# Where a hybrid encoder layer scales its softmax and splits the gate's weights, and how it loads p

## The chip, the core and the metric

The kernel runs on one core of a Trainium2 chip. A core has five engines with an instruction queue each: TensorE (PE in the profile, with its weight loads shown apart as PEld), VectorE (DVE), ScalarE (ACT), GpSimd (POOL) and SyncE (SP, which here only issues DMAs). Each engine works through its own queue in order; semaphores hold an instruction until what it needs is there. The metric is the device time of one execution in microseconds (us).

## The reference

One encoder layer on x (1024 tokens, width 1024), everything in float32:

```python
u = x @ w_in                                   # rq, rk, rv, rg, aq, ak, av
y_ret = retention(rq, rk, rv) -> group norm -> * silu(rg)      # 8 heads, both directions, chunks of 128
y_att = windowed_gqa(aq, ak, av, sink)         # 8 query heads, 2 key heads, +-128 tokens, softmax with a sink
h = LN1(alpha * x + concat(y_ret, y_att) @ w_out)
ffn = (silu(h @ w_gate) * (h @ w_up)) @ w_down                 # hidden width 2816
out = LN2(alpha * h + ffn + sigmoid(h @ w_pg) * (p @ w_pe))    # p: 1024 x 256
```

## The kernel before

Full-precision products are made from three matmuls in a reduced format: an operand x is split into `hi` (ACT copies x into the format) and `lo` (DVE computes x - hi), and a product is hi·hi + hi·lo + lo·hi. `split` (lines 72 to 74) is the ACT and DVE pair, `mm3` (76 to 79) and `mm3c` (840 to 842) are the three matmuls. A filler step below is one `mm3` with 512 columns.

The work comes in stages. (1) First projections with all PSUM banks. (2) The mixer: five calls of `run`, whose list gives PE's order by hand: operations of attention and retention for one pair of heads, and between them `None` entries, each of which stands for a portion of filler (the remaining projection matmuls, from `queue`). First come two lists for attention pair 0 alone (4 portions, 16 filler steps; then more than 20 portions, 64 steps), then retention 0 alone (14 portions, 48 steps), then pairs 1 to 3, where retention and attention go together (28 portions, 48 steps each). In the mixer only PE's order is written by hand; a planner orders ACT, DVE, POOL and SP by its own estimate of when each operand is there, in program order where several are ready. (3) The output projection and LN1. (4) The gate products and embeddings, below. (5) The gate/up products, and (6) the down products, with the order of all engines written by hand.

Softmax (lines 476 to 501, one block of 128 queries and two heads at a time): PE makes the scores, DVE adds the position term and takes the maximum (L493), ACT takes exp with the sum (L497), DVE the reciprocal (L499) and DVE scales the tile (L501). Later PE transposes it (L509) and ACT evicts the transpose (L511). There are 32 such blocks, so 64 scales.

The presplit (lines 535 to 583) prepares operands for stage 4: w_pg in seven combinations (a fast product scheme with seven in place of eight block products, 4 row blocks each, 28 in all), w_pe (4) and p (4). Each is loaded into a tile `pre`, some are summed in place (L561, 16 sums), split into a tile `pro` (two buffers) and stored to DRAM (`pgd`, `ped`, `ptd`). It begins with retention 0: `run` takes one of its 36 steps after each portion of filler. A block's two loads are in the same step as its first split.

Stage 4 computes seven products (`product`, L851 to 863; each with four rows k of 128 tokens and four weight blocks kt that `stream` loads from `pgd` into eight buffers of tags `w` and `u`) and sixteen embeddings (`embed`, L868 to 883): a load of p (L872, tile `p`, two buffers, 256 KB), six matmuls, a sigmoid of the gate's sum (L878), a product (L879) and an addition to `accs` (L881). Four embeddings follow the second product, eight are put between the rows of the last one, and four follow it. PE's order here is the planner's. Tiles of tag `ln` (two buffers) are used by `t_sums` before, which makes sums of h, and by the weights of stage 5 after (L952).

Tile `raw` has two buffers, through which most weights come before they are split: `w_mt` (filler tiles), `w_rv` (eight loads, L322, in the first list of the mixer).

Of the kernel before, what the change touches and what calls it, by code (L numbers as in the profile page):

```python
# [9 lines left out]
F32 = mybir.dt.float32  # L10
F32R = mybir.dt.float32r
AF = mybir.ActivationFunctionType
ALU = mybir.AluOpType
# [27 lines left out]
def layer(tc, xT, xn, w_first, w_mt, w_rv, w_out, w_pg, w_pe, pT, w_gu, w_dn,  # L41
# [30 lines left out]
    def split(raw, hi, lo):  # L72
        act.activation(hi, raw, AF.Copy)  # L73
        dve.tensor_tensor(lo, raw, hi.bitcast(F32), ALU.subtract)  # L74

    def mm3(o, lh, ll, rh, rl, start, stop):
        pe.matmul(o, lh, rh, start=start, stop=False)  # L77
        pe.matmul(o, lh, rl, start=False, stop=False)  # L78
        pe.matmul(o, ll, rh, start=False, stop=stop)  # L79

    last = {}

# [386 lines left out]
    class Attention:  # L469
# [6 lines left out]
        def scores(self, n):  # L476
            i, qs = self.i, self.qs
            hh, j = divmod(n, 4)
            if j == 0:
                self.st[hh] = bt([P, 4, 4, 2], "st", 2)  # L480
            st_ = self.st[hh]
            lo, hi = span(n)
            nk = (hi - lo) * P
            tc0 = C_BASE + (lo - n + 1) * P
            qc = slice(n * P, (n + 1) * P)
            sc = self.sc[n] = [bt([P, NKT + 4], "sc", NSC) for _ in range(2)]
            for g in range(2):
                pool.tensor_copy(sc[g][:, nk:nk + 1], skb[:, 2 * i + g:2 * i + g + 1])  # L488
            for g in range(2):
                b = bank("s")  # L490
                pe.matmul(b[:, :nk], qs[g][:, qc], k1[g][:, lo * P:hi * P], start=True, stop=False)
                pe.matmul(b[:, :nk], qs[g][:, qc], kz[g][:, lo * P:hi * P], start=False, stop=True)  # L492
                dve.tensor_tensor_reduce(sc[g][:, :nk], cst[:, tc0:tc0 + nk], b[:, :nk], slope(i, g),  # L493
                                         skb[:, 2 * i + g:2 * i + g + 1], ALU.add, ALU.max, st_[:, 0, j, g:g + 1])
            dve.tensor_scalar(st_[:, 1, j, :], st_[:, 0, j, :], -1.0, None, ALU.mult)  # L495
            for g in range(2):
                act.activation(sc[g][:, :nk + 1], sc[g][:, :nk + 1], AF.Exp, bias=st_[:, 1, j, g:g + 1],  # L497
                               accum_out=st_[:, 2, j, g:g + 1])
            dve.reciprocal(st_[:, 3, j, :], st_[:, 2, j, :])  # L499
            for g in range(2):  # L500
                dve.tensor_scalar(sc[g][:, :nk], sc[g][:, :nk], st_[:, 3, j, g:g + 1], None, ALU.mult)  # L501

        def turn(self, n):
            lo, hi = span(n)
# [27 lines left out]
    ped = dr.tile([2, 2, P, 2, HF], F32, name="ped")  # L532
    ptd = dr.tile([4, P, 2, HF], F32, name="ptd")

    def presplit():

        raw = [a_tile([P, 2, HF], "pre", "A1") for _ in range(2)]
        ops = [a_tile([P, 2, HF], "pro", "A1", F32R) for _ in range(2)]
        n = [0]

        def put(x, dst):
            o = ops[n[0] % 2]
            n[0] += 1
            split(x, o[:, 0, :], o[:, 1, :])
            sp.dma_start(dst, o.bitcast(F32))

        def load(k):
            for j in range(2):
                sp.dma_start(raw[j], w_pg[j, k])

        def gate_steps(k):

            (a11, a21), (a12, a22) = ([raw[j][:, i, :] for i in range(2)] for j in range(2))
            tt = dve.tensor_tensor

            def s(p, x, *sums):
                def f():
                    if p == 1:
                        load(k)
                    for a in sums:  # L560
                        tt(*a)  # L561
                    put(x, pgd[p - 1, k])
                return f

            return [s(1, a11), s(4, a22), s(2, a12), s(5, a22, (a22, a21, a22, ALU.add)),
                    s(7, a21, (a21, a11, a21, ALU.subtract)), s(6, a11, (a11, a22, a11, ALU.subtract)),
                    s(3, a12, (a12, a12, a11, ALU.subtract))]

        def pe_steps(h):
            def f(q):  # L570
                if q == 0:
                    sp.dma_start(raw[h], w_pe[h].rearrange("p (q c) -> p q c", q=2))
                put(raw[h][:, q, :], ped[h, q])
            return [lambda q=q: f(q) for q in range(2)]

        def p_steps(j):
            def f():
                x = raw[j // 2][:, j % 2, :]
                for i in range(2):
                    sp.dma_start(x[:, i * 2 * P:(i + 1) * 2 * P], pT[2 * j + i])  # L580
                put(x, ptd[j])
            return [f]

        return [f for k in range(4) for f in gate_steps(k)] + [f for h in range(2) for f in pe_steps(h)] + \
            [f for j in range(4) for f in p_steps(j)]

    side = []

# [32 lines left out]
    def run(steps, total):  # L621

        shares = steps.count(None)
        done = n = 0
        for f in steps:
            if f is None:
                n += 1
                take(total * n // shares - done)
                done = total * n // shares
                if side:  # L630
                    side.pop(0)()
            else:
                f[0](*f[1:])

    F = None
    with tc.manual_schedule(engines={mybir.EngineType.PE}):
        enqueue([mtile(0, ev_av), proj_rv(), *project(1), *project(2), *project(3), gate(0), gate(1), gate(2), gate(3)])
        a = Attention(0, ytile(1))
        sco, trn, val = (lambda n: (a.scores, n)), (lambda n: (a.turn, n)), (lambda n: (a.values, n))
        run([F, F, sco(0), F, sco(1), F], 16)  # L640
        run([F, (av_turn, 0), F, trn(0), (av_turn, 1), F, sco(2), F, trn(1), F, sco(3), F, val(0), val(1), F, trn(2), F,
             sco(4), F, trn(3), F, sco(5), F, val(2), val(3), F, trn(4), F, sco(6), F, trn(5), F, sco(7), F, val(4), val(5),
             F, trn(6), F, trn(7), F, val(6), val(7), F], 64)
        side.extend(presplit())
        r = Retention(0, ytile(0))
        K, C, N = (lambda q: (r.keys, q)), (lambda q: (r.kv, q)), (lambda q: (r.norm, q))
        Q, X = (lambda q: (r.scores, q)), (lambda q: (r.turn, q))
        Y = lambda hh, k: (r.out, hh, (2 * k, 2 * k + 1))
        run([K(0), F, C(0), K(1), F, C(1), K(2), F, Q(0), C(2), K(3), F, C(3), (r.scan,), F, F, F,
             Y(0, 0), F, Y(0, 1), N(0), F, Q(1), F, F, Y(1, 0), F, Y(1, 1), N(1), F, F], 48)  # L650
        for i in range(1, NPAIR):
            if i == 2:
                while side:
                    side.pop(0)()
            X0, X1 = X(0), X(1)
            r = Retention(i, ytile(2 * i))
            a = Attention(i, ytile(2 * i + 1))
            run([K(0), Q(0), F, X0, F, C(0), F, X1, K(1), F, C(1), sco(0), F,
                K(2), F, C(2), sco(1), F, K(3), F, trn(0), sco(2), F, C(3), (r.scan,), F, trn(1), F,
                sco(3), F, val(0), val(1), F, trn(2), Y(0, 0), F, sco(4), F, Y(0, 1), N(0), trn(3), F, sco(5), F,  # L660
                val(2), val(3), Q(1), F, trn(4), F, F, sco(6), F, trn(5), F, Y(1, 0), F, sco(7), F, val(4), val(5), F,
                Y(1, 1), N(1), trn(6), F, trn(7), F, F, val(6), val(7)], 48)
        run([F, X(0), F, X(1), F, F], 16)
# [192 lines left out]
    def four(k):  # L856
        return [bank(t) for t in sets[k]]

    def product(p, banks, first, stat, side=()):

        w = [stream(pgd[p - 1, kt]) for kt in range(4)]
        for k in range(4):
            c = slice(k * P, (k + 1) * P)
            for kt in range(4):
                mm3c(banks[k], stat[:, 0, kt, c], stat[:, 1, kt, c], w[kt][:, 0, :], w[kt][:, 1, :], first and kt == 0, kt == 3)
            if k < len(side):
                side[k]()

    def embed(t, h, x, wpe, tag):

        pt = ct([P, 2, 2 * P], "p", 2, F32R)
        sp.dma_start(pt.bitcast(F32), ptd[t // 2][:, :, (t % 2) * 2 * P:(t % 2 + 1) * 2 * P])  # L872
        b2 = bank(tag)
        for q in range(2):
            c = slice(q * P, (q + 1) * P)
# [19 lines left out]
    to_hT(4)  # L895
    to_hT(5)
    X = four("a")
    product(1, X, True, HB[0, 0], [lambda t=t: to_hT(t) for t in (6, 7)])
    s1 = [r[:, i * HF:(i + 1) * HF] for r in (rawt(2 * HF), rawt(2 * HF)) for i in range(2)]
    for k in range(4):  # L900
        act.activation(s1[k], X[k], AF.Copy)
# [15 lines left out]
    product(4, Y, False, TT[4])  # L917
    add4(s1, s1, Y)
    wpe = [stream(ped[1, q]) for q in range(2)]
    both_ = [pair_of(lambda k=k: embed(k, 1, s1[k], wpe, "mm"), lambda k=k: embed(4 + k, 1, c22[k], wpe, "s")) for k in range(4)]  # L920
    product(3, Z, False, HB[1, 1], both_)
    wpe0 = [stream(ped[0, q]) for q in range(2)]
    for k in range(4):
# [545 lines left out]
```

## Time and profile before

| | |
|---|---|
| Median of three runs | 1227.47 us (1227.15 to 1230.7) |
| Profiled execution, whole | 1230.34 us |
| Its span, first to last instruction | 1228.6 us |
| PE busy | 1201.0 us, 98% of the span |
| DVE, ACT, POOL busy | 751.0, 480.3, 364.4 us |
| Mean granted clock of TensorE | 0.993 |

The profile is of one execution. "L73" is line 73 of the kernel; tile names are the program's, with buffer numbers left out (`bmm`, `bs`, `bt`, `bo` are PSUM banks of four tags). A row such as `PE bt L370 <- DVE kv L388: 3.3, 2, 2.4` says that instructions of line 370 on PE waited for line 388 on DVE: in total, how often, the longest. A row of the timeline gives start, length, engine, line, operation, output and input tiles, shape, count and, in brackets, the idle time of the engine just before it with what ended it. A matmul's length is longer than the distance between two starts, since matmuls are pipelined; the distance is what one costs.

### The profile page before, as it was taken

To read this page: it belongs to the slowest core of one execution; us is meant where nothing else is said; L and a number is where in the kernel's file an instruction comes from. 1 tells how busy PE (TensorE), PEld (TensorE's weight loads), DVE (VectorE), ACT (ScalarE), POOL (GpSimd) and SP (SyncE) were. 2 spreads that over 40 slices of the span, in tenths; PEclk is the share of its full clock that TensorE was granted. 3 is DMA by queue.
4 is the path that set the end of the run, shared out by engine and by line. 5 is a ranking of instruction groups with operands and counts; after the bars stand their busy time and mean duration, and the time that the engine had idled before them with its cause. 6 is when DMAs were issued, how large, how long until landed. Compare 5 with 4: busy or idle time off the path is not lost.

```text
span 1228.6 us, 16503 instructions
## 1 busy us (share of the span) xinstructions
PE 1201.0 (98%) x5939; PEld 993.8 (81%) x5939; DVE 751.0 (61%) x1326; ACT 480.3 (39%) x896; POOL 364.4 (30%) x342
## 2 busy tenths in 40 slices
PE   9999989999999999999999999999999999999996
PEld 7888878788887888787788888888888888888885
DVE  5542869766755396944755544555545556875677
ACT  5633336544565114301433232332323334562453
POOL 2000010201110020000556656456465523034232
PEclk9999999999999999999999999999999999999999
DMA  6311545710103314566532133322233149999976
GB/s 253 95 35 52 206 165 230 257 35 18 35 18 121 102 52 159 201 205 220 208 129 78 71 110 129 129 78 82 99 129 129 69 147 288 387 277 218 256 175 197
DMA packets 69970, 179.50 MB, mean 146 GB/s; under 512 B 8064, under 2 KB 13312, under 8 KB 69888
## 3 DMA queue, kind: packets, MB, share of 16 engines
q1 hardware_dynamic: 61248, 161.66, 37.1%
q0 software_dynamic: 8640, 16.78, 7.7%
q8 instruction: 47, 0.77, 0.2%
q14 instruction: 35, 0.29, 0.1%
HBM read 125.72 MB, written 47.45 MB: 141 GB/s over the span
## 4 chain that ended last, share of the span: by engine, by line
PE 89%; DVE 5%; DMA 3%; issue 1%; ACT 1%; POOL 1%; DVEq 0%; SPq 0%; ACTq 0%; POOLq 0%
PE bmm L77 6%; PE bmm L79 5%; PE bmm L78 5%; PE bs L840 5%; PE bs L841 5%; PE bs L842 5%; PE bmm L840 5%; PE bmm L842 5%; PE bmm L841 5%; PE bt L840 5%; PE bt L842 5%; PE bt L841 5%; PE bo L842 4%; PE bo L840 4%; PE bo L841 4%; PE bo L521 1%
## 5 line engine op out<-in xcount | busy, mean ns | idle before, releaser
L77 PE MATMUL bmm<-H,w 128*128 128x512 f32 x240 | 100.5, 419 | 1.0 <-DVE rkq L225 0.6
L79 PE MATMUL bmm<-H,w 128*128 128x512 f32 x240 | 94.4, 393 | 0.0
L78 PE MATMUL bmm<-H,w 128*128 128x512 f32 x240 | 94.2, 392 | 0.0
L960 POOL TENSOR_TENSOR H<-ln 128x512 f32<-128x512 f32 x22 | 28.9, 1314 | 190.0 <-DMA ln<-in_w_gu 190.0
L990 POOL TENSOR_TENSOR ev<-ev 128x512 f32<-128x512 f32 x33 | 54.9, 1663 | 94.4 <-DVE ev L1005 38.8
L74 DVE TENSOR_TENSOR w<-raw,w 128x512 fp32r<-128x512 f32 x64 | 50.4, 795 | 50.7 <-ACT w L73 50.7
L488 POOL COPY sc<-skb 128x1 f32<-128x1 f32 x64 | 16.8, 271 | 207.3 <-PE bt L509 146.7
L74 DVE TENSOR_TENSOR w<-H,w 128x512 fp32r<-128x512 f32 x44 | 37.4, 850 | 62.8 <-ACT w L73 62.8
L994 POOL TENSOR_TENSOR ev<-ev,ev 128x512 f32<-128x512 f32 x44 | 62.4, 1428 | 2.6
L988 ACT ACTIVATE ev<-ev 128x512 f32<-128x512 f32 x33 | 20.9, 632 | 104.5 <-DVE ev L1005 104.5
L74 DVE TENSOR_TENSOR u<-H,u 128x512 fp32r<-128x512 f32 x47 | 37.2, 791 | 38.1 <-ACT u L73 37.8
L77 PEld LDWEIGHTS bmm<-H,w 128*128 128x128 f32 x240 | 45.3, 189 | 10.9 <-DVE rkq L225 1.5
L79 PEld LDWEIGHTS bmm<-H,w 128*128 128x128 f32 x240 | 45.1, 188 | 10.2
L497 ACT ACTIVATE sc<-sc,st 128x385 f32<-128x385 f32 (+1 forms) x64 | 37.2, 583 | 38.6 <-DVE st L495 38.4
L493 DVE CUSTOM_DVE_ANT_0 sc<-cst,bs,skb 128x384 f32<-128x384 f32 (+1 forms) x64 | 35.1, 574 | 25.9 <-PE bs L492 25.9
L78 PEld LDWEIGHTS bmm<-H,w 128*128 128x128 f32 x240 | 45.4, 189 | 6.1
L73 ACT ACTIVATE w<-raw 128x512 fp32r<-128x512 f32 x64 | 39.3, 623 | 26.5 <-PE bmm L79 10.1
L73 ACT ACTIVATE u<-H 128x512 fp32r<-128x512 f32 x47 | 29.6, 631 | 40.0 <-PE bs L842 11.3
L712 POOL TENSOR_TENSOR stt<-stt,cst 128x1 f32<-128x1 f32 x8 | 11.6, 1455 | 97.8 <-DVE stt L711 97.8
L73 ACT ACTIVATE pro<-pre 128x512 fp32r<-128x512 f32 x36 | 22.6, 627 | 41.9 <-DMA pre<-in_w_pg 11.9
L455 POOL TENSOR_TENSOR sm<-sm,cst 128x8 f32<-128x8 f32 x8 | 13.5, 1690 | 84.6 <-DVE sm L454 84.6
L964 POOL TENSOR_TENSOR H<-raw,H 128x512 f32<-128x512 f32 x22 | 37.8, 1716 | 0.0
(805 smaller groups left out, 3759.0 us busy)
## 6 DMA issues: line engine op xcount, KB each, us to landing
ad<-ev SPq DMA_DIRECT2D x33, 512.0 KB, 2.8
pgd<-pro SPq DMA_DIRECT2D x28, 512.0 KB, 2.9
raw<-in_w_gu SPq DMA_DIRECT2D x22, 512.0 KB, 4.4
ln<-in_w_gu SPq DMA_DIRECT2D x22, 512.0 KB, 3.6
raw<-ad SPq DMA_DIRECT2D x40, 256.0 KB, 5.5
ln<-ad SPq DMA_DIRECT2D x37, 256.0 KB, 6.2
H<-in_w_dn SPq DMA_DIRECT2D x33, 256.0 KB, 6.9
raw<-in_w_mt SPq DMA_DIRECT2D x14, 512.0 KB, 3.7
```

Source lines behind the costliest of these rows:

```text
L73: act.activation(hi, raw, AF.Copy)
L74: dve.tensor_tensor(lo, raw, hi.bitcast(F32), ALU.subtract)
L77: pe.matmul(o, lh, rh, start=start, stop=False)
L78: pe.matmul(o, lh, rl, start=False, stop=False)
L79: pe.matmul(o, ll, rh, start=False, stop=stop)
L497: act.activation(sc[g][:, :nk + 1], sc[g][:, :nk + 1], AF.Exp, bias=st_[:, 1, j, g:g + 1], accum_out=st_[:, 2, j, g:g + 1])
L840: pe.matmul(o, lh, rh, start=start, stop=False, skip_group_check=True)
L841: pe.matmul(o, lh, rl, start=False, stop=False, skip_group_check=True)
L842: pe.matmul(o, ll, rh, start=False, stop=stop, skip_group_check=True)
L964: pool.tensor_tensor(s[3], a(0, 1), s[0], ALU.subtract)
L990: pool.tensor_tensor(c[:, 1, :], c[:, 0, :], c[:, 1, :], ALU.mult)
L994: pool.tensor_tensor(self.ev[dst][:, 0, :], left, right, op)
```

## The change

Four things. The scale of the softmax moves from DVE to ACT. The presplit is in two parts: the 8 splits of w_pe and p come first, in the attention-only lists, through tile `raw` and a `pro` buffer of another tag; the gate's 28 follow from retention 0 on, with the loads in a step of their own, an empty step after them, and each split and sum given a dependency without a semaphore on the latest filler matmul, so that the planner puts it behind that matmul. The loads of p for the last twelve embeddings are made for two embeddings at once into the `ln` buffers, and the order of the eight embeddings within the last product is changed to match. The first product runs over kt outside and over rows k inside.

```diff
+    def behind(ins):
+        tc.add_manual_dep(ins.ins, recent[0], mybir.DependencyInfo(
+            mybir.DependencyClass.NoSync, mybir.DependencyReason.DATA), reason="order")
+        return ins
...
-                dve.tensor_scalar(sc[g][:, :nk], sc[g][:, :nk], st_[:, 3, j, g:g + 1], None, ALU.mult)
+                act.activation(sc[g][:, :nk], sc[g][:, :nk], AF.Copy, scale=st_[:, 3, j, g:g + 1])
...
+    def put(x, o, dst):
+        behind(act.activation(o[:, 0, :], x, AF.Copy))
+        behind(dve.tensor_tensor(o[:, 1, :], x, o[:, 0, :].bitcast(F32), ALU.subtract))
+        sp.dma_start(dst, o.bitcast(F32))
+
+    def presplit_small():
+        o = a_tile([P, 2, HF], "pro", "A0", F32R)
+        hold = {}
+        def load(n):
+            r = hold[n] = rawt(2 * HF)
+            if n < 2:
+                for j in range(4):
+                    sp.dma_start(r[:, j * 2 * P:(j + 1) * 2 * P], pT[4 * n + j])
+            else:
+                sp.dma_start(r, w_pe[n - 2])
+        def step(n, j):
+            put(hold[n][:, j * HF:(j + 1) * HF], o, ptd[2 * n + j] if n < 2 else ped[n - 2, j])
+        return [f for n in range(4) for f in (lambda n=n: load(n), None, lambda n=n: step(n, 0), None, None,
+                                              lambda n=n: step(n, 1))]
...
             def s(p, x, *sums):
                 def f():
-                    if p == 1:
-                        load(k)
                     for a in sums:
-                        tt(*a)
-                    put(x, pgd[p - 1, k])
+                        behind(dve.tensor_tensor(*a))
+                    put(x, ops[n[0] % 2], pgd[p - 1, k])
+                    n[0] += 1
                 return f
-            return [s(1, a11), s(4, a22), s(2, a12), ...
+            return [lambda: load(k), None, s(1, a11), s(4, a22), s(2, a12), ...
...
+        side.extend(presplit_small())
         a = Attention(0, ytile(1))
...
-        side.extend(presplit())
+        assert not side
+        side.extend(presplit_gate())
         r = Retention(0, ytile(0))
...
+        for kt in range(4 if outer else 0):
+            for k in range(4):
+                c = slice(k * P, (k + 1) * P)
+                mm3c(banks[k], stat[:, 0, kt, c], stat[:, 1, kt, c], w[kt][:, 0, :], w[kt][:, 1, :], first and kt == 0, kt == 3)
+            if kt < len(side):
+                side[kt]()
...
+    def load_p(j):
+        ptile[j] = ct([P, 2, HF], "ln", 2, F32R)
+        sp.dma_start(ptile[j].bitcast(F32), ptd[j])
...
-        pt = ct([P, 2, 2 * P], "p", 2, F32R)
-        sp.dma_start(pt.bitcast(F32), ptd[t // 2][:, :, (t % 2) * 2 * P:(t % 2 + 1) * 2 * P])
+        if ptile:
+            if t % 2 == 0:
+                load_p(t // 2)
+            pt = ptile[t // 2][:, :, (t % 2) * 2 * P:(t % 2 + 1) * 2 * P]
+        else:
+            pt = ct([P, 2, 2 * P], "p", 2, F32R)
+            sp.dma_start(pt.bitcast(F32), ptd[t // 2][:, :, (t % 2) * 2 * P:(t % 2 + 1) * 2 * P])
...
+    ptile[-1] = None
-    both_ = [pair_of(lambda k=k: embed(k, 1, s1[k], wpe, "mm"), lambda k=k: embed(4 + k, 1, c22[k], wpe, "s")) for k in range(4)]
+    both_ = [pair_of(lambda t=t, x=x: embed(t, 1, x[t % 4], wpe, "mm"), lambda t=t, x=x: embed(t + 1, 1, x[t % 4 + 1], wpe, "s"))
+             for t, x in ((0, s1), (4, c22), (2, s1), (6, c22))]
```

More of the change, by code (lines that the diff above doesn't have):

```diff
@@ L74, in split @@
         dve.tensor_tensor(lo, raw, hi.bitcast(F32), ALU.subtract)
+    recent = [None]
     def mm3(o, lh, ll, rh, rl, start, stop):
@@ L78, in mm3 @@
         pe.matmul(o, lh, rl, start=False, stop=False)
-        pe.matmul(o, ll, rh, start=False, stop=stop)
+        recent[0] = pe.matmul(o, ll, rh, start=False, stop=stop).ins.name
+    def behind(ins):
+        tc.add_manual_dep(ins.ins, recent[0], mybir.DependencyInfo(
+            mybir.DependencyClass.NoSync, mybir.DependencyReason.DATA), reason="order")
+        return ins
     last = {}
@@ L533, in layer, with presplit_gate @@
     ptd = dr.tile([4, P, 2, HF], F32, name="ptd")
-    def presplit():
+    def put(x, o, dst):
[16 more added lines that the diff above has]
+                                              lambda n=n: step(n, 1))]
+    def presplit_gate():
         raw = [a_tile([P, 2, HF], "pre", "A1") for _ in range(2)]
@@ L539, in presplit @@
         n = [0]
[L541 to L545, printed above, removed]
         def load(k):
@@ L549, in load, with steps @@
                 sp.dma_start(raw[j], w_pg[j, k])
-        def gate_steps(k):
+        def steps(k):
             (a11, a21), (a12, a22) = ([raw[j][:, i, :] for i in range(2)] for j in range(2))
-            tt = dve.tensor_tensor
             def s(p, x, *sums):
                 def f():
-                    if p == 1:
-                        load(k)
                     for a in sums:
-                        tt(*a)
-                    put(x, pgd[p - 1, k])
+                        behind(dve.tensor_tensor(*a))
+                    put(x, ops[n[0] % 2], pgd[p - 1, k])
+                    n[0] += 1
                 return f
-            return [s(1, a11), s(4, a22), s(2, a12), s(5, a22, (a22, a21, a22, ALU.add)),
+            return [lambda: load(k), None, s(1, a11), s(4, a22), s(2, a12), s(5, a22, (a22, a21, a22, ALU.add)),
                     s(7, a21, (a21, a11, a21, ALU.subtract)), s(6, a11, (a11, a22, a11, ALU.subtract)),
                     s(3, a12, (a12, a12, a11, ALU.subtract))]
[L569 to L585, printed above, removed]
+        return [f for k in range(4) for f in steps(k)]
     side = []
@@ L630, in run @@
                 if side:
-                    side.pop(0)()
+                    (side.pop(0) or (lambda: None))()
             else:
@@ L652, in layer @@
             if i == 2:
-                while side:
-                    side.pop(0)()
+                assert not side, len(side)
             X0, X1 = X(0), X(1)
@@ L857, in four, with product @@
         return [bank(t) for t in sets[k]]
-    def product(p, banks, first, stat, side=()):
+    def product(p, banks, first, stat, side=(), outer=False):
         w = [stream(pgd[p - 1, kt]) for kt in range(4)]
-        for k in range(4):
+        for kt in range(4 if outer else 0):
[4 more added lines that the diff above has]
+                side[kt]()
+        for k in range(0 if outer else 4):
             c = slice(k * P, (k + 1) * P)
@@ L867, in product @@
                 side[k]()
+    ptile = {}
+    def load_p(j):
+        ptile[j] = ct([P, 2, HF], "ln", 2, F32R)
+        sp.dma_start(ptile[j].bitcast(F32), ptd[j])
     def embed(t, h, x, wpe, tag):
-        pt = ct([P, 2, 2 * P], "p", 2, F32R)
-        sp.dma_start(pt.bitcast(F32), ptd[t // 2][:, :, (t % 2) * 2 * P:(t % 2 + 1) * 2 * P])
+        if ptile:
[5 more added lines that the diff above has]
+            sp.dma_start(pt.bitcast(F32), ptd[t // 2][:, :, (t % 2) * 2 * P:(t % 2 + 1) * 2 * P])
         b2 = bank(tag)
@@ L897, in layer @@
     X = four("a")
-    product(1, X, True, HB[0, 0], [lambda t=t: to_hT(t) for t in (6, 7)])
+    product(1, X, True, HB[0, 0], [lambda t=t: to_hT(t) for t in (6, 7)], True)
     s1 = [r[:, i * HF:(i + 1) * HF] for r in (rawt(2 * HF), rawt(2 * HF)) for i in range(2)]
```

## The prediction

> **What bounds the kernel now.** I read the page first: its busy times say which engine sets the length.
>
> ```profile
> span 1228.6 us, 16503 instructions
> PE 1201.0 (98%) x5939; PEld 993.8 (81%) x5939; DVE 751.0 (61%) x1326; ACT 480.3 (39%) x896; POOL 364.4 (30%) x342
> ```
>
> TensorE (PE) is busy for all but 27.6 us, and the change takes away no matmul. What it can gain is idle time of PE and whatever slows PE down. So the second view is the waits of PE, longest first (total, times, longest):
>
> ```profile
> PE bt L370 <- DVE kv L388: 3.3, 2, 2.4
> PE bt L384 <- DVE kdec L373: 2.6, 2, 1.9
> PE bmm L840 <- DMA w<-pgd: 2.4, 1, 2.4
> PE bmm L77 <- DMA p<-ptd: 1.9, 1, 1.9
> PE bs L77 <- DMA p<-ptd: 1.7, 2, 1.1
> ...
> PE bo L77 <- DMA p<-ptd: 0.7, 1, 0.7
> ```
>
> Three places: the mixer (kv, kdec), one gate product (w), and the embeddings (p: 1.9 + 1.7 + 0.7 = 4.3 us). The third view puts them into stages: retention 0 alone, pair 1, pair 2, pair 3, and the stretch with the late p. The columns are the length, then busy time (and count) of PE, its weight loads, DVE, ACT and POOL, then the granted clock, DMA share and GB/s.
>
> ```profile
> 121.00:169.40 48.40, 47.51 (x277) 39.77 (x276) 36.22 (x74) 14.73 (x25) 1.66 (x1) 1.00 0.50 184
> 169.40:243.00 73.60, 67.11 (x450) 56.33 (x448) 62.74 (x157) 41.87 (x97) 11.81 (x23) 0.98 0.66 236
> 243.00:309.00 66.00, 64.72 (x451) 54.75 (x450) 43.63 (x123) 27.68 (x71) 11.73 (x24) 1.00 0.10 32
> 309.00:382.00 73.00, 72.36 (x488) 61.26 (x488) 44.45 (x125) 45.43 (x86) 8.28 (x18) 1.00 0.14 44
> 571.20:596.00 24.80, 20.51 (x79) 15.24 (x78) 14.61 (x20) 6.46 (x11) 8.77 (x6) 0.93 0.57 200
> ```
>
> Pair 1 and pair 2 issue the same matmuls, and pair 1 takes 7.6 us longer: 6.5 us idle against 1.3, and a clock below 1. It is the pair that shares DVE and ACT with the presplit, DVE being 85% busy there and 66% in pair 2. The clock matters because a long wait is paid twice. Matmul starts before and after the wait of 1.9 us for p:
>
> ```profile
> 570.28 0.39 PE L840 MATMUL bo<-u,h 128*128 128x512 f32 x1
> 570.51 0.39 PE L841 MATMUL bo<-u,h 128*128 128x512 f32 x1
> ```
>
> and
>
> ```profile
> 574.30 0.63 PE L77 MATMUL bmm<-u,p 128*128 128x512 f32 x1
> 574.73 0.63 PE L78 MATMUL bmm<-u,p 128*128 128x512 f32 x1
> ```
>
> They start 0.23 us apart before it and 0.43 after it. In the stretch row above the clock averages 0.93 over 24.8 us, and 0.07 x 24.8 = 1.7 us are lost that way; pair 1 has 0.02 x 73.6 = 1.5. So a wait near 2 us costs some 3.5, and two waits near 1 us are cheaper than one near 2.
>
> [...]
>
> **The change part by part.**
>
> Softmax scale. 64 DVE operations go, 64 ACT operations come. The rows are the DVE scale that goes and, as the nearest for what comes, ACT's exp over the same tile (one column more); then the presplit's two engines:
>
> ```profile
> L501 DVE TENSOR_SCALAR sc<-sc,st 128x384 f32<-128x384 f32 (+1 forms) x64 | 22.9, 399 | 0.5
> ```
>
> ```profile
> L497 ACT ACTIVATE sc<-sc,st 128x385 f32<-128x385 f32 (+1 forms) x64 | 37.2, 583 | 38.6 <-DVE st L495 38.4
> ```
>
> ```profile
> L73 ACT ACTIVATE pro<-pre 128x512 fp32r<-128x512 f32 x36 | 22.6, 627 | 41.9 <-DMA pre<-in_w_pg 11.9 <-DMA pgd<-pro 10.2 <-DVE pre L561 6.9
> L74 DVE TENSOR_TENSOR pro<-pre,pro 128x512 fp32r<-128x512 f32 x36 | 24.6, 687 | 21.4 <-ACT pro L73 21.2
> ```
>
> DVE loses 22.9 us, a quarter of it (5.7) in each run that has attention. ACT gains 64 x 0.58 = 37 us, 9.3 per run: pair 3, its fullest, goes from 45.4 to 54.7 of 73 us. The chain of one softmax gets about 0.4 us longer (two scales of 0.58 for two of 0.40), plus one more hand-over from DVE to ACT, with a wait at the head of ACT: behind it queue exps, evictions (L511, L222) and filler splits (L73), for which PE waits in turn. What hides it is the distance from scale to transposes. The first block of pair 1, the tightest that I found:
>
> ```profile
> 189.07 0.61 DVE L501 TENSOR_SCALAR sc<-sc,st 128x256 f32<-128x256 f32 x2
> ```
>
> ```profile
> 191.54 0.38 PE L509 MATMUL bt<-cst,sc 128*128 128x128 f32 x2
> ```
>
> Its scale ends at 189.7, 1.9 us ahead of its transposes, and that cover is more than the 0.4. I cost the move at 0 on PE, with ends of +2 (such a block 1 us late in two pairs) and -1 (DVE's relief in pairs 2 and 3, of their 1.3 + 0.6 us idle).
>
> Presplit. Of its 36 splits 8 (two weights of p and p itself) move to the attention-only run, where they cost 8 x 0.69 = 5.5 us of DVE and 8 x 0.63 = 5 of ACT. The 28 of the gate and their 16 sums stay in retention 0 and pair 1, at one step per filler portion, as before: 28 splits and 8 load or empty steps fill the same 36 portions. New are that a load is issued two portions ahead of its first split, and that a split stands in the engines' order behind the last filler product. The latter is an order of the planner and no wait on the chip. ACT's waits show what the earlier load is worth: `pro` idles 11.9 us on loads and 10.2 on stores (the row above), all at the head of ACT, with DVE's split behind it (21.2). Do these reach PE? At pair 1's start:
>
> ```profile
> 175.52 0.91 PE L384 MATMUL bt<-rv,kdec 128*128 128x128 f32 x6 [1.89 <-DVE kdec L373]
> 180.63 0.41 PE L370 MATMUL bt<-cst,rkq 128*128 128x128 f32 x2 [2.38 <-DVE kv L388]
> ```
>
> ```profile
> 173.89 1.15 DVE L456 TENSOR_TENSOR ym<-ym,sm 128x512 f32<-128x512 f32 x1 [1.04 <-POOL sm L455]
> ...
> 178.67 1.28 DVE L74 TENSOR_TENSOR pro<-pre,pro 128x512 fp32r<-128x512 f32 x2
> 179.87 0.61 DVE L388 TENSOR_TENSOR kv<-bt,cst 128x256 f32<-128x256 f32 x2
> ```
>
> The 2.38 has two presplit operations right ahead of kv: 1.3 us of it goes if they stand elsewhere. What is late next is the same kv, by the remaining 1.1 us. The 1.89 comes from POOL's power step in the norm ahead of kdec, and stays. So of pair 1's 6.5 us I take 1.3, the clock's 1.5 (the pair of long waits is broken), and 1.5 of the 2.2 us in short waits, as DVE loses 5.7 us of scales and up to 5.5 of splits there; of retention 0's 0.9 I take 0.7, the other kdec wait (2.6 - 1.9). Sum -5.0. Ends: all idle of both stages and the clock gone, -8.9; +2, a new order with one more wait like the 1.89.
>
> Its price elsewhere: the 8 early splits load through `raw`, two buffers, which six loads of `w_rv` need at the same time, and the first of the four holds one until portion 6. One load through a single buffer takes 2.7 (landing) + 0.63 + 0.69 and some 0.3 of hand-overs, 4.3 us; the first can start when the split below, the last of the tile before, gives its buffer free:
>
> ```profile
> DMA to landing us min/median/max: 2.4/2.7/4.2
> ```
>
> ```profile
> 38.95 0.81 DVE L74 TENSOR_TENSOR w<-raw,w 128x512 fp32r<-128x512 f32 x1 [1.61 <-ACT w L73]
> ```
>
> ```profile
> 67.08 0.40 PE L77 MATMUL bmm<-qq,H 128*128 128x512 f32 x1
> ```
>
> 39.8 + 6 x 4.3 = 65.6 us, and PE wants the sixth at 67.1. Cover 1.5 us, less if ACT's evictions come between. I take +0.5, ends 0 and +5 (3.5 late, 1.5 of clock). SP's queue gets ten loads and eight stores there in place of none, in a stretch where the DMA engines are near idle; 0.
>
> p in pairs. Of the twelve later embeddings each two share one load of 512 KB in place of two of 256, through two `ln` buffers. From the DMA view:
>
> ```profile
> w<-pgd SPq DMA_DIRECT2D x14, 512.0 KB, 5.8
> ```
>
> ```profile
> p<-ptd SPq DMA_DIRECT2D x16, 256.0 KB, 4.4
> ```
>
> 12 embedding matmuls are 12 x 0.23 = 2.7 us and a product row the same. Loads 1 and 2 find `ln` free long before. For 3 and 4 the buffer falls free 8.2 us (a product row, two embeddings, a product row) before use, against 5.8: hidden. The fifth (reload for t = 4) has 5.5 us: 0.5 late. The sixth has 2.7: 3.1 late unless the planner puts the first gate/up unit (12 matmuls, 2.7 us) in between, as it does now: I take 1.0. Then `ln` is given up later, and SP's hand-written order has the load of the second `raw` behind the one into `ln`: 1.0. So 4.3 + 1.7 (clock) - 2.5 = -3.5. Ends: -6.0, and +0.3 (0.5 + 3.1 + 1.0 + 1.7 against 6.0).
>
> Row-outermost first product. Its last two weight loads, its first matmul, and the matmul with the wait for w:
>
> ```profile
> 468.97 1.15 SPq L851 DMA_DIRECT2D u<-pgd  x2
> ```
>
> ```profile
> 478.85 0.48 PE L840 MATMUL bmm<-w,h0a 128*128 128x512 f32 x1
> ...
> 507.84 0.47 PE L840 MATMUL bmm<-w,H 128*128 128x512 f32 x1 [2.43 <-DMA w<-pgd]
> ```
>
> No wait stands before it: its four weights are asked for by 470.1. The wait for w is 29 us later, in another product. So the step does not remove a wait; 0 here; four weight buffers fall free up to 8 us earlier. Ends: -4.1 (that wait and its 1.7 us clock go, if the planner orders it otherwise) and +2 (a like wait).
>
> Sum: 0 - 5.0 + 0.5 - 3.5 + 0 = -8.0. The profiled execution took 1230.3 us, 2.9 over the median of 1227.5; it becomes 1222.3, the median 1219.5.
>
> **The rivals.**
> (a) ScalarE becomes the bound: slower. Place: pairs 1 to 3, ACT waiting at the head for each reciprocal. Against: 28 filler portions per pair with other work to put between, and 54.7 of 73 us. For: its exps already wait 2.0 us each for DVE in 19 places:
>
> ```profile
> ACT sc L497 <- DVE st L495: 38.4, 19, 4.5
> ```
>
> Eight hand-overs per pair at 2.0 fill pair 3 to 70.7 of 73; at 3.5 it is 82.7, 9.7 more than now, and pair 1 with 41.9 + 9.3 + 28 - 5 has 74.2 against 69.3 us, 4.9 more: 1219.5 + 14.6 = 1234. With h per hand-over the two lose 54.7 + 8h - 73 and 46.2 + 8h - 69.3; the gain of 8 is eaten at h = 3.1.
> (b) The waits only move: ACT still blocked by loads in pair 1 (gain 1.5), the late p at its bad end: 1227.5 - 1.5 + 0.3 + 0.5 = 1227.
> (c) The `raw` buffers hold PE up by their bad end: 1219.5 + 4.5 = 1224.
> (d) Everything goes, the wait at 507.84 too: -8.9 - 6.0 - 4.1 + 0.5: 1209.
> (e) The slow stretches stay though the waits go, being no work of theirs: 1.5 + 1.7 us less gain, 1222.7. Against it: the stretch shown follows its wait at once. [...]
>
> **How the numbers follow.** Forecast 0.50, (a) 0.14, (b) 0.14, (c) 0.07, (d) 0.12, (e) 0.03. A measurement here tells 0.3%, 3.7 us, from no change. Faster: 0.50 + 0.12 + 0.03 and most of (c), 0.70; same: (b) and the rest of (c), 0.16; slower: (a), 0.14. Range 1210 to 1230, which leaves out (a) and half of (d).
>
> **What would show it.** No wait of PE for p over 1.2 us, and at most one slow stretch there. kv's wait near 1 us, kdec's still 1.9; pair 1 near 69 us. `pro` waits for loads gone from ACT. About 37 us more ACT on the scale's line, no PE wait for it. A wait for `raw`'s data between 60 and 70 us would be (c). Wrong: new waits of PE for ACT, or for w in the products after 500 us.

## The result, and the profile after

The changed kernel takes 1229.37 us (median; 1225.9 to 1232.8) against 1228.59 us for the kernel before, measured beside it: a ratio of 1.0004, 95% interval 0.9991 to 1.0017. Nothing that can be measured was gained or lost, where 8 us of gain were forecast. The profiled execution of it took 1232.8 us as a whole, the slowest of its fifteen.

The first lines of the page of the changed kernel:

```profile
span 1231.0 us, 16420 instructions
PE 1202.4 (98%) x5939; PEld 995.7 (81%) x5939; DVE 732.0 (59%) x1262; ACT 510.1 (41%) x960; POOL 366.7 (30%) x342
```

DVE lost 19 us and ACT gained 30: the 64 scales took 22.9 us on DVE and take 34.0 on ACT. PE stands still 28.6 us, one more than before, but in other places. The waits of PE in the changed kernel (total, times, longest):

```profile
PE bmm L849 <- ACT u L73: 7.6, 1, 7.6
PE bt L392 <- DVE kdec L381: 2.4, 3, 1.3
PE bmm L849 <- DMA w<-pgd: 2.3, 1, 2.3
PE bt L378 <- ACT y L471: 1.6, 1, 1.6
...
PE bmm L79 <- ACT qq L73: 0.9, 1, 0.9
...
PE bt L378 <- DVE kv L396: 0.5, 1, 0.5
PE bs L79 <- DMA ln<-ptd: 0.3, 1, 0.3
```

The four waits for p (4.3 us) are down to one of 0.3, kv's 3.3 us to 0.5, and the wait for w is where it was. New at the head is a single wait of 7.6 us, for ACT's split of `u`.

Lines have moved: L849 is L840 before, L378 and L392 are L370 and L384, L79 is L77, L889 loads p, L910 stores the sums `accs` to DRAM (`zd`), and L981 (L952 before) loads the weights of the gate/up stage. Where the two profiled executions drift apart, by the first instruction of each stage:

| us from the span's start | before | after | difference | change since the row above |
|---|---|---|---|---|
| first transposes of `av` | 62.5 | 65.1 | +2.6 | |
| keys of retention 0 | 121.0 | 125.3 | +4.3 | +1.7 |
| keys of pair 1 | 169.4 | 172.1 | +2.7 | -1.6 |
| keys of pair 2 | 243.0 | 242.7 | -0.3 | -3.0 |
| keys of pair 3 | 308.9 | 308.1 | -0.8 | -0.5 |
| first transposes of h | 439.55 | 438.65 | -0.9 | -0.1 |
| first embedding | 502.5 | 501.6 | -0.9 | 0 |
| first `bs<-H,w` matmul of gate/up, past the long wait | 601.4 | 603.5 | +2.1 | +3.0 |
| end of the span | 1228.6 | 1231.0 | +2.4 | +0.3 |

So the mixer gave 5.2 us, the `raw` buffers cost 1.7, the stretch from the embeddings to the gate/up products lost 3.0 instead of gaining, and 2.6 were lost in the first 10 us, where the two kernels do the same (told at the end). The mixer's stages, to be read beside the rows of the prediction (the columns are the same):

```profile
121.00:170.00 49.00, 49.00 (x301) 41.71 (x300) 32.44 (x66) 12.80 (x23) 2.03 (x1) 1.00 0.48 167
170.00:243.00 73.00, 69.06 (x461) 57.93 (x459) 58.85 (x143) 47.34 (x110) 14.41 (x23) 0.98 0.52 195
243.00:309.00 66.00, 65.22 (x458) 55.23 (x458) 39.54 (x107) 36.02 (x88) 11.46 (x25) 1.00 0.08 25
```

In pair 1 the idle time of PE fell from 6.5 us to 3.9, and the stretch of retention 0 has none left.

Where does the 7.6 us wait come from? Followed back: PE waits for a split on ACT, ACT for the load of the second `raw` tile of gate/up weights. These are PE's rows (start, length), and ACT's:

```profile
593.56 0.80 PE L849 MATMUL bmm<-h0a,u 128*128 128x512 f32 x1 [7.61 <-ACT u L73]
594.15 0.63 PE L850 MATMUL bmm<-h0a,u 128*128 128x512 f32 x1
594.57 0.63 PE L851 MATMUL bmm<-h0a,u 128*128 128x512 f32 x1
```

```profile
592.87 0.63 ACT L73 ACTIVATE u<-raw 128x512 fp32r<-128x512 f32 x1 [10.74 <-DMA raw<-in_w_gu]
```

And this is SP's queue in the same kernel; the length of a row reaches from the first to the last of the DMAs it counts:

```profile
577.25 0.32 SPq L889 DMA_DIRECT2D ln<-ptd  x1
579.97 0.33 SPq L981 DMA_DIRECT2D ln<-in_w_gu  x1
580.40 6.20 SPq L910 DMA_DIRECT2D zd<-acc  x4
586.69 0.38 SPq L981 DMA_DIRECT2D raw<-in_w_gu  x1
```

The load that PE waits for is issued at 586.69. Ahead of it on SP stand a load into `ln`, which could only start once the last pair of p but one was read out of its buffer (the last matmul that reads it starts at 579.55), and then four stores of `acc`, each of which waits for DVE's last addition to it; the last of these additions runs from 584.97 to 586.25. In the kernel before the same load was issued 7.4 us earlier, ahead of the last embeddings' loads and stores:

```profile
579.29 0.38 SPq L952 DMA_DIRECT2D raw<-in_w_gu  x1
```

Behind the wait the matmul starts lie 0.43 us apart until 597.1 and 0.23 after it; the granted clock is 0.53 from 593.5 to 597.2 us, and 0.47 x 3.7 = 1.7 us more. The wait with what follows it costs 9.3 us. It eats what the embeddings gained (9.3 - 3.0 = 6.3 us) and 3.0 of the mixer's 5.2.

### The profile page after: what moved, and what is told of

It is laid out like the page before. It is cut to its first block, busy times and chain, and to the rows that moved or that the text cites. A ratio compares the mean times of both kernels' runs of the same rounds, so it can differ in the third digit from the quotient of the medians.

```text
span 1231.0 us, 16420 instructions
## 1 busy us (share of the span) xinstructions
PE 1202.4 (98%) x5939; PEld 995.7 (81%) x5939; DVE 732.0 (59%) x1262; ACT 510.1 (41%) x960; POOL 366.7 (30%) x342
## 4 chain that ended last, share of the span: by engine, by line
PE 88%; DVE 4%; DMA 3%; ACT 2%; issue 1%; POOL 1%; SPq 0%; DVEq 0%; ACTq 0%; POOLq 0%
PE bmm L79 6%; PE bmm L80 5%; PE bmm L81 5%; PE bmm L849 5%; PE bmm L850 5%; PE bmm L851 5%; PE bs L849 5%; PE bs L851 5%; PE bs L850 5%; PE bo L851 4%; PE bo L850 4%; PE bo L849 4%; PE bt L849 4%; PE bt L851 4%; PE bt L850 4%; PE bo L529 1%
## 5 line engine op out<-in xcount | busy, mean ns | idle before, releaser
L79 PE MATMUL bmm<-H,w 128*128 128x512 f32 x240 | 100.6, 419 | 0.6 <-ACT H L73 0.6
L74 DVE TENSOR_TENSOR w<-H,w 128x512 fp32r<-128x512 f32 x44 | 39.6, 900 | 62.7 <-ACT w L73 62.7
L79 PEld LDWEIGHTS bmm<-H,w 128*128 128x128 f32 x240 | 45.4, 189 | 9.8 <-ACT H L73 1.5
L74 DVE TENSOR_TENSOR u<-raw,u 128x512 fp32r<-128x512 f32 x26 | 31.9, 1226 | 10.4 <-ACT u L73 10.4
```

## The experiments

The theory: each of the parts gained about what was forecast, and one load that is held up on SP took it all back, 9.3 us. The rivals: the gains were never there (the waits only moved); the loss belongs to the first product's order or the mixer's new order; or a wait next in line takes the place of the 7.6 us, whatever SP does. Ratios are to the kernel before on the same chip, with 95% intervals.

**x1_raw_first: the changed kernel, the two `raw` loads of the first gate/up pair issued ahead of the first load into `ln`.** Nothing else moves.

```diff
-        def load(self, m):
-            for i in range(2):
+        def load(self, m, which=(0, 1)):
+            for i in which:
                 r = rawt(2 * HF) if i == 0 else ct([P, D], "ln", 2)
...
-            if p == 1:
+            if p == 1 and n:
                 pr.load(m)
+            elif p == 1:
+                for mm_, which in (((0, (0,)), (1, (0,)), (0, (1,))), ((1, (1,)),))[m]:
+                    pr.load(mm_, which)
```

> The changed kernel with one thing moved: for the first gate/up pair, the second load into raw is issued ahead of the first load into ln. Theory 1 (SP's queue): that load stood behind a load that waits for ln and behind four stores of zd, so TensorE's wait of 7.6 us and its slow clock (1.7 us) go; 9.3 us less than the changed kernel, 8.5 less than before, ratio to before 0.993. Theory 2 (the DMA engines are full there, or ScalarE and VectorE bring the operand late anyway): the load lands hardly earlier or the next operand is late instead, less than 3 us gained, ratio 0.998 to 1.001.

1222.35 us, ratio 0.9951 (0.9935 to 0.9968): 7.0 us less than the changed kernel's median, 6.5 by the two ratios, and 7.6 less than x4 below, which takes the time of the changed kernel and ran beside this run on one chip. SP's queue in it:

```profile
565.78 0.33 SPq L981 DMA_DIRECT2D raw<-in_w_gu  x1
...
577.20 0.33 SPq L981 DMA_DIRECT2D ln<-in_w_gu  x1
577.66 6.14 SPq L910 DMA_DIRECT2D zd<-acc  x4
583.90 0.37 SPq L981 DMA_DIRECT2D ln<-in_w_gu  x1
```

The `raw` load goes out 21 us earlier (18 if the 2.8 us are taken off by which this profile is ahead at the load into `ln`); the rest of the queue looks as in the changed kernel, four stores and all, and now nobody waits for what stands behind them. The stretch from 577 to 604 us, first of the changed kernel, then of this one:

```profile
577.00:604.00 27.00, 19.09 (x76) 15.03 (x76) 16.96 (x18) 10.96 (x19) 12.63 (x8) 0.87 0.52 184
```

```profile
577.00:604.00 27.00, 26.93 (x119) 22.00 (x118) 17.55 (x21) 10.52 (x17) 11.85 (x8) 1.00 0.47 168
```

7.9 us of idle time became 0.1, and the clock 1.00. The 9.3 us expected were read from one execution, the slowest of fifteen; 7.0 arrive. The waits of PE in this kernel offer a place for the rest:

```profile
PE bmm L849 <- DMA w<-pgd: 2.7, 1, 2.7
...
PE bs L849 <- DVE ev L1034: 2.0, 2, 1.2
```

The second row, 2.0 us for DVE in later gate/up units, isn't in the changed kernel. It may be that the long wait had given DVE the time to get ahead; no run shows that. So the load's place in SP's queue is shown to be the cause of the long wait, and where the remaining 2 us went is not shown.

**z1_raw_first_again: the same kernel**, as the partner of a run below on the same chip.

> x1_raw_first once more, beside the next on the same chip: 0.995.

1222.75 us, 0.9953 (0.9937 to 0.9969): the same.

**x2_p_only: the kernel before with p in pairs alone** (the loads and the order of the eight embeddings).

```diff
+    def load_p(j):
+        ptile[j] = ct([P, 2, HF], "ln", 2, F32R)
+        sp.dma_start(ptile[j].bitcast(F32), ptd[j])
...
+    ptile[-1] = None
-    both_ = [pair_of(... embed(k, ...), ... embed(4 + k, ...)) for k in range(4)]
+    both_ = [pair_of(... embed(t, ...), ... embed(t + 1, ...)) for t, x in ((0, s1), (4, c22), (2, s1), (6, c22))]
```

> The kernel before with p in pairs alone (softmax, presplit and first product as before). Theory 1: the waits for p go (6.0 us with the clock) and the wait for the second gate/up unit comes (9.3 us), 3 us slower, ratio 1.0025. Theory 2 (that wait needs another part of the change): 6 us faster, ratio 0.995.

1234.58 us, 1.0044 (1.0028 to 1.0059): slower, alone. Its waits of PE:

```profile
PE bmm L840 <- ACT u L73: 7.8, 1, 7.8
PE bt L370 <- DVE kv L388: 3.2, 2, 2.4
PE bt L384 <- DVE kdec L373: 2.8, 2, 2.3
PE bmm L840 <- DMA w<-pgd: 2.6, 1, 2.6
```

The wait for `u` comes with this part and with nothing else; the mixer's waits are those of before, and those for p are gone. Where -3.5 us had been forecast, this part by itself is worth +5.0 in the median, 2 more than was expected of this run.

**x3_mixer_only: the changed kernel with p loaded as before and the loops of the first product as before** (so the scale on ACT and the presplit in two parts).

```diff
-    product(1, X, True, HB[0, 0], [lambda t=t: to_hT(t) for t in (6, 7)], True)
+    product(1, X, True, HB[0, 0], [lambda t=t: to_hT(t) for t in (6, 7)])
...
(load_p and the order of the embeddings as in the kernel before)
```

> The kernel before with the softmax scale on ScalarE and the presplit in two parts alone. Theory 1 (the two stage sums of the trace hold): 5.2 us won in retention 0 to pair 3 and 1.5 lost on the w_rv loads, 3.5 us faster, ratio 0.997, and the late p as before (4.3 us of waits). Theory 2 (the shorter pairs are an accident of that one execution): ratio 0.999 to 1.001.

1225.87 us, 0.9972 (0.9957 to 0.9986), 3.8 us faster. From the keys of retention 0 to the transposes of h its profile takes 312.1 us, the kernel before 318.5: 6.4 us gained there; ahead of it the `raw` buffers took back 1.7 (60.2 us from the `av` transposes to retention 0, against 58.5). p makes PE wait 1.7 + 1.2 + 0.3 us, 3.2 against 4.3 before, and there is no wait for `u`.

**x4_rows_inside: the changed kernel with the loops of the first product as before, rows k of tokens outside and weight blocks kt inside** (the first of the two edits above, alone). A "row" in the recorded texts on this step is a block kt of the weights' rows.

> The changed kernel with the rows inside again in the first gate product. Both theories: no wait stood before that product in either kernel, so the same as the changed kernel within 1 us, ratio to before 1.000 to 1.001. Were the order worth something, over 2 us slower than the changed kernel.

1229.95 us, 1.0004 (0.9989 to 1.002): the order of the first product's loops does nothing that can be measured, and the 7.9 us for `u` and 3.1 for w stand as in the changed kernel.

**y1_softmax_only: the kernel before with the scale on ACT alone.**

```diff
-                dve.tensor_scalar(sc[g][:, :nk], sc[g][:, :nk], st_[:, 3, j, g:g + 1], None, ALU.mult)
+                act.activation(sc[g][:, :nk], sc[g][:, :nk], AF.Copy, scale=st_[:, 3, j, g:g + 1])
```

> The kernel before with the softmax scale on ScalarE alone. Theory 1 (most of what the mixer won comes from the split presplit and its earlier loads; the scale alone relieves VectorE by 5.7 us a run but leaves ScalarE blocked on loads): 0 to 1.5 us faster, ratio 0.999 to 1.000, the two long waits at the start of pair 1 stay. Theory 2 (VectorE's relief is what won): 4 us faster, ratio 0.9965.

1224.75 us, 0.9972 (0.9956 to 0.9989), 3.9 us faster: a miss, since no more than 1.5 us was expected. Pair 1 of this kernel:

```profile
172.50:244.00 71.50, 67.16 (x450) 56.36 (x449) 56.76 (x139) 48.84 (x113) 11.46 (x23) 0.98 0.68 237
```

PE stands still 4.3 us there against 6.5. DVE, at 62.7 of 73.6 us before, is relieved by 6 us, and that comes through to PE: kdec's waits fall from 2.6 us in all to 0.9, while kv's 2.4 us stays.

**y2_presplit_only: x3 with the scale left on DVE.**

> The kernel before with the presplit in two parts alone. Theory 1: 3 us faster or a little more, ratio 0.9975, the wait for kv under 1 us. Theory 2: less than 1.5 us, ratio 0.999 to 1.000.

1226.05 us, 0.9971 (0.9956 to 0.9986), 2.6 us faster. Retention 0 to the transposes of h takes 312.3 us, 6.2 less than before and no more than x3's 312.1 with both. Its waits of PE from 170 to 250 us have lost kv's:

```profile
PE bt L392 <- DVE kdec L381: 2.2, 2, 1.3
PE bt L378 <- ACT y L471: 1.6, 1, 1.6
```

So beside the spread presplit the scale's move is worth nothing that can be measured. Alone the two parts give 3.9 and 2.6 us, together 3.8, with intervals of some 2 us to each side. By the profiles they don't take the same waits (y1 shortens kdec's and keeps kv's, y2 does the reverse), but both relieve pair 1, and there the gains don't add up: it takes 73.5 us before, 71.3 in y1, 70.0 in y2 and 69.5 in x3.

**z2_presplit_no_behind: y2 without the dependency on the latest filler product** (the loads and the order of the steps stay).

```diff
     def behind(ins):
-        tc.add_manual_dep(ins.ins, recent[0], mybir.DependencyInfo(
-            mybir.DependencyClass.NoSync, mybir.DependencyReason.DATA), reason="order")
         return ins
```

> y2_presplit_only without the dependency on the latest filler product: the presplit in two parts, its loads in a step of their own, splits placed freely by the planner. Theory 1 (the load two portions ahead is what frees ScalarE and VectorE): the same as y2_presplit_only, ratio 0.997. Theory 2 (the place behind the filler product is what does it): as before, 0.9995 to 1.001, with kv and kdec waits near 2 us again.

1227.42 us, 0.9986 (0.9971 to 1.0). Its waits from 170 to 250 us:

```profile
PE bt L390 <- DVE kdec L379: 3.7, 2, 3.0
PE bt L376 <- DVE kv L394: 1.7, 1, 1.7
```

kv's wait is back and kdec's is longer than in the kernel before. In the profiles y2 gains 6.2 us in the mixer and this one 1.1 (317.4 us), but this execution was the slowest of its twelve, and a good part of the 5.1 us between them is its slower clock (granted 0.95 in pair 1, 1.00 in y2): pair 1 takes 4.1 us longer than in y2, of which only 1.6 are idle time of PE (6.1 against 4.5). The medians, each against the kernel before, lie 1.5 us apart, with intervals that overlap. That the place in DVE's order carries a part of the presplit's gain is likely from the waits and not shown by the times.

**y3_raw_first_small_late: x1, the eight early splits begun one list later**, past the loads of `w_rv`.

```diff
-        side.extend(presplit_small())
         a = Attention(0, ytile(1))
...
         run([F, F, sco(0), F, sco(1), F], 16)
+        side.extend(presplit_small())
...
-        return [... (lambda n=n: load(n), None, lambda n=n: step(n, 0), None, None,
+        return [... (lambda n=n: load(n), None, lambda n=n: step(n, 0), None,
```

> The changed kernel with the raw load ahead (as in x1_raw_first) and with the small presplit begun after the first list of the mixer, so that its loads come behind the eight of w_rv, one empty step less each. Theory (the small loads hold a raw buffer that w_rv needs): the waits for qq at 70 us go, 1.4 us less than x1_raw_first, ratio to before 0.994. Rival (ScalarE's evictions make them late): the waits stay, the same as x1_raw_first.

1219.99 us, 0.9935 (0.9911 to 0.996). The wait for `qq` near 70 us is gone, and from the `av` transposes to retention 0 it takes 58.8 us, against 60.2 in the changed kernel and 58.5 before. That takes away 1.4 of the 1.7 us of the `raw` buffers and shows where they came from. The medians of this run and x1 are not told apart by their intervals.

**y4_second_product_outer: x1 with the second product's weights in the outer loop too**, for the wait for w, which lies in that product.

```diff
-    product(2, X, False, HB[1, 0], steps[0:4])
+    product(2, X, False, HB[1, 0], steps[0:4], True)
```

> As x1_raw_first, with the second gate product row-outermost as well as the first. Theory (the wait of 2.7 us for w after the embeddings is for a load that stands until the second product gives its buffer free at its very end; outermost, that buffer is free about 3 us earlier): the wait and its slow clock, 2.7 + 1.7 us, go, ratio to before 0.9915. Rival (bandwidth: three loads at once): the wait shrinks by less than 1 us and the slow clock stays, ratio 0.995.

1221.89 us, 0.9945 (0.9925 to 0.9964): no different from x1's 0.9951 by this measurement, though the wait of 2.7 us is gone from the list of waits and only one of 0.7 for w is left.

**z4_second_outer_again: the same kernel, on one chip with z1.**

> y4_second_product_outer once more, beside z1_raw_first_again on the same chip. If the wait for w of 2.7 us and a slow stretch that always follows it go: 3.7 us less than z1. If the slow stretch follows a wait of that size only in some executions: about 2 to 2.7 us less. If something else is late instead: the same.

1220.88 us, 0.9935 (0.9914 to 0.9956), beside z1's 0.9953: 1.9 us less, with intervals that still overlap. That it is worth about 2 us is likely and not shown.

**y5_all: x1 with both, the early splits later and the second product turned.**

> The changed kernel with the raw load ahead, the small presplit begun after the first list, and the second product row-outermost as well. If the three are independent: x1_raw_first less 1.4 us for the raw buffer and less 2.0 to 3.7 us for the wait for w and its clock, 1218 to 1219 us, ratio to before 0.991 to 0.992. If another wait takes the place of the last: 0.9935, as y3_raw_first_small_late.

1217.37 us, 0.9904 (0.9879 to 0.9928): 11 us faster than the kernel before, a little more than the 1218 to 1219 us expected of three independent gains. Its page and its longest waits of PE:

```profile
span 1217.4 us, 16420 instructions
```

```profile
PE bt L392 <- DVE kdec L381: 2.5, 3, 1.3
PE bs L849 <- DVE ev L1034: 2.2, 2, 1.2
PE bt L378 <- ACT y L471: 1.6, 1, 1.6
```

No wait over 1.6 us is left. The prediction's rival (d), "everything goes", had put 1209 on it.

## Why the prediction was wrong

**The step that failed is the third term of "p in pairs"**: "`ln` is given up later, and SP's hand-written order has the load of the second `raw` behind the one into `ln`: 1.0". The place was right and the mechanism half: the load does stand behind the one into `ln`. But four stores of `acc` stood between the two as well, 6.2 us of queue, which end only with DVE's last addition. The term measured 7.6 us of wait and 1.7 of slow clock, 9.3. What was left out is the question that the part asked of other steps: what else stands ahead of it in that queue, and whom does each of those wait for? With 9.3 in place of 1.0 the forecast of -8.0 becomes +0.3, and the median moved by +0.8. That the two lie so close is in part luck: with the other terms as the profile has them (-5.2, +1.7 and -6.3, below) the sum is -0.5. That 1229.4 us lies within the stated 1210 to 1230 is no support for the forecast either: the range reached so far for (b), and no sum in it holds this wait.

The forecast had this wait in its list of what would prove it wrong ("new waits of PE for ACT"), but no rival took it up with a price of its own: the part's bad end, +0.3, held the same 1.0 us. x2 gave +5.0.

The other steps:

- **Softmax scale, 0.** Right beside the presplit (x3 and y2 are the same), wrong alone: -3.9 us (y1). The end of -1 for DVE's relief was too small; in pair 1, where DVE is 85% busy, 5.7 us less work on it took 2.2 us of idle time off PE. I had counted this relief under the presplit's short waits, and alone it does the same. Rival (a) had ACT waiting 2 to 3.5 us for each reciprocal. The groups of ACT in the changed kernel, the scale first:

```profile
L509 ACT ACTIVATE sc<-sc,st 128x384 f32<-128x384 f32 (+1 forms) x64 | 34.0, 580 | 2.5 <-DVE st L507 2.5
L505 ACT ACTIVATE sc<-sc,st 128x385 f32<-128x385 f32 (+1 forms) x64 | 37.1, 582 | 27.2 <-DVE st L503 27.1
L544 ACT ACTIVATE pro<-pre 128x512 fp32r<-128x512 f32 x28 | 17.4, 625 | 17.1 <-DMA pgd<-pro 10.9 <-DVE pre L584 5.2 <-DMA pre<-in_w_pg 0.9
```

  34 us for 64 scales (37 forecast), and 2.5 us of waiting for the reciprocal in all, 0.04 each: (a) is out. The exps wait 27 us for DVE, not 38.
- **Presplit, -5.0.** The mixer gave 5.2 us in the changed kernel's profile and 6.2 in y2's. Of its terms: kv's 2.4 us went altogether and a wait of 1.6 for ACT's `y` came up in its place, 0.8 gained where 1.3 were forecast; kdec's one wait of 1.9 became three of 2.4 in all, the longest 1.3; retention 0 gave 1.6 (0.7 forecast). The 1.5 us of clock came in some executions and not in others (last section). The total was right, its parts only roughly. As forecast, `pro` hardly waits for loads any more (0.9 us in the row above, 11.9 before).
- **`raw` buffers, +0.5 with ends 0 and +5.** 1.7 us by the profile; y3 took 1.4 of it away. PE wanted the sixth split 0.9 us before it came, so the cover of 1.5 us was all used up: "less if ACT's evictions come between" was the case. ACT's splits of `w_rv` follow each other at some 4 us, as reckoned (4.3), but 9.1 us lie between those that start at 45.12 and 54.24, with thirteen evictions of projections between them.
- **p in pairs, the waits.** -4.3 - 1.7 + 0.5 + 1.0 = -4.5 forecast, -6.3 by the profile: of the fifth and sixth load 0.3 us is left. (The 0.5 for the fifth is 0.3 by its own numbers, 5.8 less 5.5.)
- **Row-outermost first product, 0.** Right (x4): weight blocks kt outside or inside, no difference.
- **The rivals.** (b), "the waits only move", comes closest by its time, 1227, and not by its reason: the gain was there and was lost in another stage.

## What to carry to other kernels

Before a tile is moved into a buffer that later loads use, list the whole queue that issues those loads, stores too, and ask for each entry ahead of the load what it waits for: here one load stood behind four stores that waited for another engine, 6.2 us of queue, and issuing it ahead of them and of a load into `ln` gave 7.0 us without any other change. Two parts that relieve the same engine in the same stage may gain less together than their sum (here 3.9 and 2.6 us alone, 3.8 together), so try them together before adding. For a presplit or other side work on an engine that also feeds PE, a place in the order behind a product is worth trying beside an earlier load; here the two medians, 1.5 us apart, don't settle what it gives.

## What the runs showed of the hardware

**A slow stretch of the clock after waits of 1 to 3 us comes in one execution and not in another.** The changed kernel and x1 have the same code up to the gate/up loads and the same waits of PE at the start of pair 1. First the changed kernel, with the 8 us from 182.00 (its columns as above), then x1 with the 8 us at the same place:

```profile
182.01 0.44 PE L378 MATMUL bt<-cst,rkq 128*128 128x128 f32 x2 [1.62 <-ACT y L471]
...
184.04 2.07 PE L392 MATMUL bt<-rv,kdec 128*128 128x128 f32 x8 [0.89 <-DVE kdec L381]
```

```profile
182.00:190.00 8.00, 7.10 (x31) 6.05 (x32) 6.36 (x19) 2.44 (x5) 0.00 (x0) 0.79 0.64 249
```

```profile
179.41 0.44 PE L378 MATMUL bt<-cst,rkq 128*128 128x128 f32 x2 [1.62 <-ACT y L471]
...
181.45 1.16 PE L392 MATMUL bt<-rv,kdec 128*128 128x128 f32 x8 [0.89 <-DVE kdec L381]
```

```profile
179.00:187.00 8.00, 6.69 (x41) 5.67 (x42) 7.81 (x24) 3.79 (x10) 0.00 (x0) 1.00 0.72 258
```

The waits are 1.32 (not shown), 1.62 and 0.89 us in both; the granted clock is 0.79 in the one and 1.00 in the other, 0.21 x 8 = 1.7 us. The eight transposes of L392 take 2.07 us and 1.16. The wait for w shows the like: after 2.69 us in x1 the starts lie 0.43 us apart, after 2.60 us in z2 0.23, and there the granted clock is 1.00 from 500 to 520 us:

```profile
503.51 0.73 PE L849 MATMUL bmm<-w,H 128*128 128x512 f32 x1 [2.69 <-DMA w<-pgd]
504.03 0.63 PE L850 MATMUL bmm<-w,H 128*128 128x512 f32 x1
504.46 0.63 PE L851 MATMUL bmm<-w,H 128*128 128x512 f32 x1
```

```profile
509.77 0.47 PE L847 MATMUL bmm<-w,H 128*128 128x512 f32 x1 [2.60 <-DMA w<-pgd]
510.07 0.40 PE L848 MATMUL bmm<-w,H 128*128 128x512 f32 x1
510.31 0.39 PE L849 MATMUL bmm<-w,H 128*128 128x512 f32 x1
```

Behind the waits of 7.61 us in the changed kernel and 7.95 in x4 the slow stretch came both times: starts lie 0.43 us apart up to 597.1 us in both, with a granted clock of 0.53 from 593.5 to 597.2 us in the changed kernel. The prediction took a wait near 2 us for a sure 3.5, and it is only a chance of that; how large a chance these runs don't show. What decides whether a slow stretch follows was not tried.

**The start differs too.** In the profiled execution of the changed kernel the first matmuls run slow for longer. Its rows, then those of the kernel before:

```profile
5.63 0.63 PE L79 MATMUL bs<-H,w 128*128 128x512 f32 x1
...
9.47 0.61 PE L80 MATMUL bo<-H,w 128*128 128x512 f32 x1
```

```profile
5.04 0.40 PE L77 MATMUL bs<-H,w 128*128 128x512 f32 x1
```

Starts are 0.43 us apart up to 9.5 us from the span's start, in the kernel before only up to 4.7; some eleven matmuls at 0.2 us more are the 2.2 of the 2.6 us by which the table above begins. The granted clock reads 1.00 from 0 to 12 us in both, so that this is the clock is not shown. z1 has the same code there, and its starts are 0.23 us apart from 5.15 us on. Such differences, with the slow stretches, are of the size by which executions of one kernel lie apart here (1225.9 to 1232.8 us), so two profiles are to be compared stage by stage, with the clock and the distance between matmul starts beside each.
